# Forgetting attention: head keys, low parts and extra rows loaded from SyncE's queue, and each pair's values loaded behind the value matmuls

## The chip, the cores and the metric

The kernel runs on one core of one Trainium2 chip. The metric is device time in microseconds (us) of that core. A core has TensorE (PE, matrix products into PSUM), VectorE (DVE), ScalarE (ACT) and GpSimd (POOL), which all work out of an on-chip memory of 128 partitions, and SyncE (SP), which here does nothing but start transfers. Each engine works through its own instructions in a fixed order, and an instruction whose inputs or buffers are not ready holds up everything behind it on that engine. Data moves between device memory and the chip by DMA; the transfers of one core share 16 DMA engines. A transfer is started by an instruction on SP, ACT or POOL, and the profile keeps a queue for each of them apart.

## The reference

One inference step of a small decoder: a prompt of 512 tokens and eight sample sequences of four tokens each, 1,024 features wide. A layer with gated linear attention is followed by one with forgetting attention, and each has a feed-forward half before and behind its mixer. The change lies in the forgetting attention. Its keys, values and forget gates are computed once; for the prompt it is ordinary causal attention with a bias from the running sum F of the log forget gates:

```python
s = jnp.einsum('bqhd,bkhd->bhqk', qi, k).astype(jnp.float32) * scale
s = s + (Fi[:, :, :, None] - Ft[:, :, None, :])
s = jnp.where(kpos[None, :] <= qpos[:, None], s, -jnp.inf)
p = jax.nn.softmax(s, axis=-1)
return jnp.einsum('bhqk,bkhd->bqhd', p.astype(v.dtype), v)
```

There are 16 heads of 64 features. A sample sequence attends, with the same formula, over two pages of 128 cached rows, which a page table picks, and over its own four rows. Behind either kind of attention stand the gate `sigmoid(og)` and the output projection `w_o`.

## The kernel before

**The whole.** Nearly all of the run is dense products on PE. Most operands are split into a high and a low part, and each product is made in three passes (high by high, low by high, high by low; L176 to L178), so that float32 accuracy comes out of a faster format ("fp32r" in the profile). The forgetting-attention stage is the function `fox` (L1155 on): it projects queries and gates (`fq`, `fg`), runs the attention loop, and then the output projection (`fwo`). The loop, L1383 to L1409, takes some 146 us of the run.

**The loop.** It has 18 steps. Step i makes the scores and probabilities of prompt head i (`head_probs`), transposes the probabilities of head i-1 (`head_turn`), and in odd steps from 3 on multiplies the values of one pair of heads (`head_values((i-3)//2)`). Woven into it is the attention of the sample sequences, one pair of sequences p in each four steps: `pair_keys` for its first and second sequence (cache blocks b = 2p and 2p+1) in the first two of them, `pair_softmax` and `pair_probs` in the others, and in the next four `pair_values` and `pair_out`. So four heads and one pair of sequences make one group, and there are four groups.

**What a pair of heads loads.** Keys, values and gates were written to scratch in device memory earlier in the run. In each even step `pair_loads(kb)` (L1314) loads for one pair of heads, one pair ahead of its use:

- `vq` (L1316, 256 KB): the values, by SP, into one of two buffers.
- `kd` (L1319, 256 KB in each of two transfers of 64 partitions): the high parts of the keys, by POOL, into one of six buffers (`hi_tile`) that the transposed cache keys `kpT` share.
- `kl` (L1321, 296 KB): the low parts of the keys, and ten more rows with the gates' sums, 74 partitions of two rows of 2 KB each, by POOL, two buffers.
- `qe` (L1323, 40 KB): ten extra rows of the queries that go with them, by POOL, two buffers.

ScalarE and, for all pairs but the first, POOL also split that pair's queries here (L1327 to L1329), into `uh` and `ul`. The scores of a head (L1344 to L1346, tiles `fs`) are, for each block of 128 queries, a product with `kd`, a product with `kl` and a product that adds the causal mask; `kd`'s comes first. ScalarE takes the exponential (L1348). Transposes of the probabilities go to PSUM at L1362 and are copied out by ScalarE (L1366) or VectorE (L1368). The value products (L1377, tiles `fo`) read `vq`; their result is gated by VectorE (L1379), rounded by ScalarE (L1380, `uh`), and POOL subtracts to get the low part (L1381, `ul`).

**What a sample sequence loads.** `pair_keys` starts four transfers of 512 KB, all by SP: two pages of keys `kp` (L1234) and two of values `vp` (L1238). PE transposes the keys in 16 products (L1245, tiles `kpT`, over two PSUM buffers that the other transposes share), VectorE (L1250) and ScalarE (L1248) copy them out, and the scores `sp` (L1227, L1258) and, later, the values `so` (L1295, L1298) follow.

**What sets the order.** The program's text gives the dependencies; a scheduler of the language fixes, when the program is built, one order of instructions for each engine, SP's and POOL's starts of transfers included. In the order listings below, the number at the end of a tile's name only tells tiles apart; the digits ahead of it are the pair of heads (`kd4`), the sequence and the page (`kp2_0`), or the head and the block of queries (`fs5_3`).

Of the kernel before, what the change touches and what calls it, by code (L numbers as in the profile page):

```python
# [9 lines left out]
F32 = mybir.dt.float32  # L10
# [8 lines left out]
P = 128  # L19
D = 1024  # L20
NB = 8
# [29 lines left out]
KX = 74  # L51
# [48 lines left out]
def trunk_kernel(ctx: ExitStack, tc: tile.TileContext, a, out, dbg=None, stop=None):  # L100
    nc = tc.nc
    V, S, G, PE, SP = nc.vector, nc.scalar, nc.gpsimd, nc.tensor, nc.sync
# [7 lines left out]
    def mm_bank(name):  # L110
        return pp.tile([P, 512], F32, tag="mm", name=name, bufs=5)
# [11 lines left out]
    def hi_tile(name, dt=F32R):  # L123
        return wp.tile([P, 1056], dt, tag="hi", name=name, bufs=6)
# [874 lines left out]
    vscr = dram.tile([TP, D], F32, name="vscr")  # L999
    khscr = dram.tile([D, TP], F32, name="khscr")  # L1000
    klscr = dram.tile([16, KX, TP], F32, name="klscr")
    qxscr = dram.tile([16, KX - 64, TP], F32, name="qxscr")
# [152 lines left out]
    def fox(after_half):  # L1155
        W = a["fox_w_qg"][0]
        with ExitStack() as es:
# [43 lines left out]
            fa = es.enter_context(tc.tile_pool(name="foxa", bufs=1))  # L1201
# [75 lines left out]
            def pair_probs(p):  # L1277
                x, xn = pst[p][3:5]
                pt_ = aux_bank(f"spT{p}")
                PE.transpose(pt_[:, 0:128], x[:, 0:128], ident)  # L1280
                PE.transpose(pt_[:, 128:256], x[:, 128:256], ident)
                PE.transpose(pt_[:, 256:384], xn[:].rearrange("p a t -> p (a t)"), ident)
                xT = rb[:, 0:512]
                S.copy(xT[:, 0:384], pt_[:, 0:384])
                pst[p].append(xT)

            def pair_values(p):
                vv, xT = pst[p][2], pst[p][5]
                po = xp.tile([P, 512], F32, tag="sp", name=f"so{p}")
                for s2 in range(2):  # L1290
                    for step in range(3):
                        for j in range(4):
                            o = po[32 * j:32 * j + 32, 256 * s2:256 * s2 + 256]
                            if step < 2:
                                PE.matmul(o, lhsT=xT[:, step * P + 32 * j:step * P + 32 * j + 32], rhs=vv[2 * s2 + step][:, 256 * j:256 * j + 256], start=step == 0, stop=False)  # L1295
                            else:
                                r = slice(32 * j, 32 * j + 32)
                                PE.matmul(o, lhsT=xT[r, 256 + 32 * j:288 + 32 * j], rhs=vnew[r, :], start=False, stop=True)  # L1298
                xo = rb[:, 0:512].rearrange("p (a d) -> p a d", d=64)
                V.tensor_tensor(out=xo, in0=po[:].rearrange("p (a d) -> p a d", d=64), in1=cf[:, F_DIAG:F_DIAG + 8].unsqueeze(2).to_broadcast([P, 8, 64]), op=ALU.mult)  # L1300
                o2 = tmp.tile([P, 128], F32, tag="acc", name=f"o2{p}", bufs=2)
                V.tensor_reduce(out=o2[:], in_=xo.rearrange("p (a b) d -> p (b d) a", b=2), axis=AX.X, op=ALU.add)
                pst[p].append(o2)
# [7 lines left out]

            hst = {}

            def pair_loads(kb):  # L1314
                vq = fa.tile([P, 4, P], F32, tag="vq", name=f"vq{kb}", bufs=2)
                SP.dma_start(out=vq[:], in_=vscr[:].rearrange("(t p) d -> p t d", p=P)[:, :, kb * P:(kb + 1) * P])  # L1316
                kd = hi_tile(f"kd{kb}")[:, 0:1024].rearrange("p (e t) -> p e t", e=2)
                for g in range(2):
                    G.dma_start(out=kd[64 * g:64 * g + 64], in_=khscr[kb * P:(kb + 1) * P].rearrange("(e p) t -> p e t", e=2))  # L1319
                kl = fa.tile([KX, 2, TP], F32R, tag="kl", name=f"kl{kb}", bufs=2)  # L1320
                G.dma_start(out=kl[:], in_=klscr[2 * kb:2 * kb + 2].rearrange("e p t -> p e t"))  # L1321
                qx = fa.tile([KX, 2, TP], F32R, tag="qe", name=f"qe{kb}", bufs=2)
                G.dma_start(out=qx[64:KX], in_=qxscr[2 * kb:2 * kb + 2].rearrange("e p t -> p e t"))  # L1323
                qs = (uh[:, kb, 0:TP], ul[:, kb, 0:TP])
                for e in range(2):
                    r, x = slice(64 * e, 64 * e + 64), slice(64 - 64 * e, 128 - 64 * e)
                    S.copy(qs[e][r], qT[r, kb])  # L1327
                    (G if kb else V).tensor_tensor(out=qs[e][x], in0=qT[r, kb], in1=qs[e][r].bitcast(F32), op=ALU.subtract)
                    S.copy(qx[0:64, e], qT[r, kb])  # L1329
                hst["v", kb], hst["k", kb] = vq, (kd, kl, qs, qx)  # L1330

            def head_probs(hd):
                kb, hh = divmod(hd, 2)
                kd, kl, qs, qx = hst["k", kb]
                gb = fa.tile([P, 1280], F32, tag="gb", name=f"gb{hd}", bufs=2)
                mx = fa.tile([P, 3, 4], F32, tag="mx", name=f"mx{hd}", bufs=3)
                for bank in BANKS:
                    ps = mm_bank(f"fs{hd}_{bank[0]}")
                    o = 0
                    for qt in bank:  # L1340
                        n = (qt + 1) * P
                        tq, one = slice(qt * P, (qt + 1) * P), slice(qt, qt + 1)
                        s_, g = ps[:, o:o + n], gb[:, base(qt):base(qt + 1)]
                        PE.matmul(s_, lhsT=qs[hh][:, tq], rhs=kd[:, hh, 0:n], start=True, stop=False)  # L1344
                        PE.matmul(s_, lhsT=qx[0:KX, hh, tq], rhs=kl[:, hh, 0:n], start=False, stop=False)
                        PE.matmul(ps[:, o + n - P:o + n], lhsT=identb[:], rhs=causb[:], start=False, stop=True)  # L1346
                        V.tensor_reduce(out=mx[:, 0, one], in_=s_, axis=AX.X, op=ALU.min)
                        S.activation(g, s_, AF.Exp, bias=mx[:, 0, one], scale=-1.0, accum_out=mx[:, 1, one])  # L1348
                        o += n
                    for qt in bank:  # L1350
                        one, g = slice(qt, qt + 1), gb[:, base(qt):base(qt + 1)]
                        V.reciprocal(out=mx[:, 2, one], in_=mx[:, 1, one])
                        V.tensor_scalar(out=g, in0=g, scalar1=mx[:, 2, one], scalar2=None, op0=ALU.mult)
                hst["g", hd] = gb
# [17 lines left out]
            def head_values(kb):  # L1372
                vq = hst["v", kb]
                po = mm_bank(f"fo{kb}")
                for kt in range(4):
                    for hh in range(2):
                        PE.matmul(po[64 * hh:64 * hh + 64, kt * P:512], lhsT=vq[:, kt, 64 * hh:64 * hh + 64], rhs=hst["p", 2 * kb + hh][kt][:], start=kt == 0, stop=kt == 3)  # L1377
                og = tmp.tile([P, TP], F32, tag="w2", name=f"og{kb}", bufs=1)
                V.tensor_tensor(out=og[:], in0=sg[kb // 2][:, kb % 2], in1=po[:], op=ALU.mult)  # L1379
                S.copy(uh[:, kb, 0:TP], og[:])  # L1380
                G.tensor_tensor(out=ul[:, kb, 0:TP], in0=og[:], in1=uh[:, kb, 0:TP].bitcast(F32), op=ALU.subtract)  # L1381

            sc_ = {}  # L1383
            for i in range(18):
                p, q = divmod(i, 4)
                if i == 0:
                    pair_loads(0)
                if i % 2 == 0 and i < 14:
                    pair_loads(i // 2 + 1)
                if i < 16:  # L1390
                    head_probs(i)
                if p and q == 0:
                    pair_values(p - 1)
                if p < 4 and q == 0:
                    sc_[0] = pair_keys(p, 0)
                if p < 4 and q == 1:
                    sc_[0]()
                    sc_[1] = pair_keys(p, 1)
                if i >= 3 and i % 2:
                    head_values((i - 3) // 2)  # L1400
                if p < 4 and q == 2:
                    sc_[1]()
                    pair_softmax(p)
                if 1 <= i < 17:
                    head_turn(i - 1)
                if p < 4 and q == 3:
                    pair_probs(p)
                if p and q == 1:
                    pair_out(p - 1)  # L1409
            V.tensor_tensor(out=oS[:], in0=oS[:], in1=sgs[:], op=ALU.mult)  # L1410
            halves(uh[:, :, TP:T], ul[:, :, TP:T], oS[:])
            out_proj("fwo", a["fox_w_o"][0], mod(1, 1, 2), after_half)

    fox(after("12", mod(1, 2, 0), mod(1, 2, 1)))
    dump("h4", h[:])
    if stop == "fox":
# [48 lines left out]
```

## Time and profile before

| | us |
|---|---|
| median of three runs | 2459.66 (2458.26 to 2464.04) |
| profiled execution, its own time | 2463.23 |
| its span, first to last instruction | 2461.4 |
| mean granted clock of PE over the span | 0.989 |
| 0 to 1850 us: PE busy | 1805.2 |
| 1850 to 1996 us, the attention loop: PE busy | 128.1 of 146 |
| 1996 to 2461 us: PE busy | 458.2 |

All times of one instruction and all waits come from the one profiled execution; the median is over separate runs. In the list of waits a row gives the engine and line that waited, what it waited for, the total in us, how many times, and the longest. A row of a timeline has the start, the duration, the engine (SPq is SP's queue), line, operation, output and inputs, and in brackets how long the engine stood idle before it and for whom. A row of a table by stretches has the stretch, its length, the busy time of PE, PE's weight loads, VectorE, ScalarE and POOL with the number of their instructions, and then PE's granted clock as a share of full speed, the mean busy share of the 16 DMA engines, and the traffic in GB/s. A row of the transfers has the tile and its source, the queue, the count, the size of one, and the median of the time from the start instruction to the landing.

### The profile page before, as it was taken

To read this page: it belongs to the slowest core of one execution; us is meant where nothing else is said; L and a number is where in the kernel's file an instruction comes from. 1 tells how busy PE (TensorE), PEld (TensorE's weight loads), DVE (VectorE), ACT (ScalarE), POOL (GpSimd) and SP (SyncE) were. 2 spreads that over 40 slices of the span, in tenths; PEclk is the share of its full clock that TensorE was granted. 3 is DMA by queue.
4 is the path that set the end of the run, shared out by engine and by line. 5 is a ranking of instruction groups with operands and counts; after the bars stand their busy time and mean duration, and the time that the engine had idled before them with its cause. 6 is when DMAs were issued, how large, how long until landed. Compare 5 with 4: busy or idle time off the path is not lost. (4 is left out here: it accounts for less than half of the span.)

```text
span 2461.4 us, 48211 instructions
## 1 busy us (share of the span) xinstructions
PE 2391.6 (97%) x20204; PEld 2244.4 (91%) x20204; DVE 1235.5 (50%) x2823; ACT 783.5 (32%) x1431; POOL 289.5 (12%) x448
## 2 busy tenths in 40 slices
PE   7999999999899999999999999999999799999999
PEld 6999999988879999999979999999896579999999
DVE  6343334557656344344585344434847656444433
ACT  4212222344534213222334322222337444222221
POOL 0000000104302010000220000000325220000000
PEclk9999999999999999999999999999999899999999
DMA  9636454213172646554247323322157742222221
GB/s 308 232 126 231 156 178 133 65 48 96 36 215 60 224 145 230 179 176 154 97 125 233 99 66 109 97 92 69 44 109 196 177 129 74 91 88 93 70 85 54
DMA packets 325519, 319.38 MB, mean 130 GB/s; under 512 B 24607, under 2 KB 276349, under 8 KB 325254
## 3 DMA queue, kind: packets, MB, share of 16 engines
q1 hardware_dynamic: 297958, 293.81, 37.4%
q0 software_dynamic: 13776, 11.87, 2.3%
q10 hardware_dynamic: 13568, 10.62, 1.4%
q8 instruction: 159, 2.61, 0.4%
q14 instruction: 58, 0.48, 0.1%
HBM read 298.17 MB, written 18.38 MB: 129 GB/s over the span
## 5 line engine op out<-in xcount | busy, mean ns | idle before, releaser
L176 PE MATMUL pa<-uh,hua 128*128 128x272 f32 x1408 | 409.5, 291 | 2.0 <-ACT uh L386 2.0
L177 PE MATMUL pa<-ul,hua 128*128 128x272 f32 x1408 | 407.7, 290 | 0.4 <-DVE ul L387 0.2
L178 PE MATMUL pb<-uh,lub 128*128 128x272 f32 x1408 | 407.5, 289 | 0.0
L176 PE MATMUL pd<-gh,hwd 128*128 128x272 f32 x1408 | 407.4, 289 | 0.0
L178 PE MATMUL pa<-uh,lua 128*128 128x272 f32 x1408 | 406.6, 289 | 0.0
L176 PE MATMUL pb<-uh,hub 128*128 128x272 f32 x1408 | 405.5, 288 | 0.0
L177 PE MATMUL pb<-ul,hub 128*128 128x272 f32 x1408 | 405.5, 288 | 0.0
L177 PE MATMUL pd<-gl,hwd 128*128 128x272 f32 x1408 | 405.5, 288 | 0.0
L178 PE MATMUL pd<-gh,lwd 128*128 128x272 f32 x1408 | 405.2, 288 | 0.0
L393 DVE SCALAR_TENSOR_TENSOR h<-pd,mods,h 128x272 f32<-128x272 f32 (+1 forms) x384 | 185.2, 483 | 255.6 <-PE pd L178 254.4
L176 PEld LDWEIGHTS pa<-uh,hua 128*128 128x128 f32 x1408 | 265.3, 188 | 15.1 <-issue 6.0
L176 PEld LDWEIGHTS pd<-gh,hwd 128*128 128x128 f32 x1408 | 265.1, 188 | 2.9 <-issue 2.9
L177 PEld LDWEIGHTS pa<-ul,hua 128*128 128x128 f32 x1408 | 265.7, 189 | 1.4 <-DVE ul L387 1.2
L177 PEld LDWEIGHTS pb<-ul,hub 128*128 128x128 f32 x1408 | 266.1, 189 | 0.0
L178 PEld LDWEIGHTS pb<-uh,lub 128*128 128x128 f32 x1408 | 265.8, 189 | 0.0
L176 PEld LDWEIGHTS pb<-uh,hub 128*128 128x128 f32 x1408 | 265.7, 189 | 0.0
L177 PEld LDWEIGHTS pd<-gl,hwd 128*128 128x128 f32 x1408 | 265.5, 189 | 0.0
L178 PEld LDWEIGHTS pd<-gh,lwd 128*128 128x128 f32 x1408 | 265.4, 188 | 0.0
L178 PEld LDWEIGHTS pa<-uh,lua 128*128 128x128 f32 x1408 | 265.4, 188 | 0.0
L446 DVE TENSOR_TENSOR g<-g,pb 128x272 f32<-128x272 f32 x176 | 77.1, 438 | 346.5 <-PE pb L178 346.3
L157 ACT CAST hua<-rua 128x1024 fp32r<-128x1024 f32 x88 | 92.2, 1048 | 462.9 <-PE pd L177 352.0
L398 POOL TENSOR_TENSOR h<-h,gs 128x32 f32<-128x32 f32 x192 | 69.5, 362 | 1230.7 <-DVE gs L396 1214.6
(497 smaller groups left out, 4173.1 us busy)
## 6 DMA issues: line engine op xcount, KB each, us to landing
adaw<-in_w_ada_dram SPq DMA_DIRECT2D x128, 512.0 KB, 6.2
rua<-in_w_ffn_up_dram SPq DMA_DIRECT2D x88, 512.0 KB, 3.8
rub<-in_w_ffn_up_dram SPq DMA_DIRECT2D x88, 512.0 KB, 3.8
rwd<-in_w_ffn_down_dram SPq DMA_DIRECT2D x88, 512.0 KB, 5.3
adah<-in_w_ada_dram SPq DMA_DIRECT2D x16, 512.0 KB, 7.9
adaw<-in_w_ada_kv_dram SPq DMA_DIRECT2D x16, 512.0 KB, 7.3
s<-in_state_gla_dram SPq DMA_DIRECT2D x16, 512.0 KB, 6.2
kp<-in_cache_k_dram SPq DMA_DIRECT2D x16, 512.0 KB, 5.7
```

What stands on the lines that cost most here:

```text
L157: S.copy(hi, src)
L176: PE.matmul(ps, lhsT=wh, rhs=xh, start=first and i == 0, stop=False)
L177: PE.matmul(ps, lhsT=wh, rhs=xl, start=False, stop=False)
L178: PE.matmul(ps, lhsT=wl, rhs=xh, start=False, stop=last and i == n - 1)
L393: V.scalar_tensor_tensor(out=h[:, m, t0:p1], in0=ps[:, 0:n], scalar=mods[:, gate + m, 0:1], in1=h[:, m, t0:p1], op0=ALU.mult, op1=ALU.add)
L398: G.tensor_tensor(out=h[:, m, TP:T], in0=h[:, m, TP:T], in1=st[:], op=ALU.add)
L446: V.tensor_tensor(out=g[:], in0=g[:], in1=pb[:, 0:HA], op=ALU.mult)
```

## The change

The transfers of `kd`, `kl` and `qe` are started by SP in place of POOL. Their tiles have the type fp32r and their source float32; the tiles are now named to the transfer as plain float32, of the same bits, so that nothing has to be converted and SP can start them. The transfer of `vq` leaves `pair_loads` and becomes a function `value_load` of its own: the values of the first two pairs are loaded in step 0, and those of pair (i+1)//2 right behind the value products of pair (i-3)//2, whose buffer they take. Sizes, buffers and all arithmetic are the same. Lines of the changed kernel: `vq` L1317, `kd` L1323, `kl` L1325, `qe` L1327, the scores L1348 to L1350, the transposes of probabilities L1366, the value products L1381; lines up to L1310 keep their numbers.

```diff
--- before.py
+++ after.py
@@ -1311,23 +1311,27 @@
 
             hst = {}
 
+            def value_load(kb):
+                if kb < NB:
+                    vq = fa.tile([P, 4, P], F32, tag="vq", name=f"vq{kb}", bufs=2)
+                    SP.dma_start(out=vq[:], in_=vscr[:].rearrange("(t p) d -> p t d", p=P)[:, :, kb * P:(kb + 1) * P])
+                    hst["v", kb] = vq
+
             def pair_loads(kb):
-                vq = fa.tile([P, 4, P], F32, tag="vq", name=f"vq{kb}", bufs=2)
-                SP.dma_start(out=vq[:], in_=vscr[:].rearrange("(t p) d -> p t d", p=P)[:, :, kb * P:(kb + 1) * P])
                 kd = hi_tile(f"kd{kb}")[:, 0:1024].rearrange("p (e t) -> p e t", e=2)
                 for g in range(2):
-                    G.dma_start(out=kd[64 * g:64 * g + 64], in_=khscr[kb * P:(kb + 1) * P].rearrange("(e p) t -> p e t", e=2))
+                    SP.dma_start(out=kd[64 * g:64 * g + 64].bitcast(F32), in_=khscr[kb * P:(kb + 1) * P].rearrange("(e p) t -> p e t", e=2))
                 kl = fa.tile([KX, 2, TP], F32R, tag="kl", name=f"kl{kb}", bufs=2)
-                G.dma_start(out=kl[:], in_=klscr[2 * kb:2 * kb + 2].rearrange("e p t -> p e t"))
+                SP.dma_start(out=kl[:].bitcast(F32), in_=klscr[2 * kb:2 * kb + 2].rearrange("e p t -> p e t"))
                 qx = fa.tile([KX, 2, TP], F32R, tag="qe", name=f"qe{kb}", bufs=2)
-                G.dma_start(out=qx[64:KX], in_=qxscr[2 * kb:2 * kb + 2].rearrange("e p t -> p e t"))
+                SP.dma_start(out=qx[64:KX].bitcast(F32), in_=qxscr[2 * kb:2 * kb + 2].rearrange("e p t -> p e t"))
                 qs = (uh[:, kb, 0:TP], ul[:, kb, 0:TP])
                 for e in range(2):
                     r, x = slice(64 * e, 64 * e + 64), slice(64 - 64 * e, 128 - 64 * e)
                     S.copy(qs[e][r], qT[r, kb])
                     (G if kb else V).tensor_tensor(out=qs[e][x], in0=qT[r, kb], in1=qs[e][r].bitcast(F32), op=ALU.subtract)
                     S.copy(qx[0:64, e], qT[r, kb])
-                hst["v", kb], hst["k", kb] = vq, (kd, kl, qs, qx)
+                hst["k", kb] = (kd, kl, qs, qx)
 
             def head_probs(hd):
                 kb, hh = divmod(hd, 2)
@@ -1385,6 +1389,8 @@
                 p, q = divmod(i, 4)
                 if i == 0:
                     pair_loads(0)
+                    value_load(0)
+                    value_load(1)
                 if i % 2 == 0 and i < 14:
                     pair_loads(i // 2 + 1)
                 if i < 16:
@@ -1398,6 +1404,7 @@
                     sc_[1] = pair_keys(p, 1)
                 if i >= 3 and i % 2:
                     head_values((i - 3) // 2)
+                    value_load((i + 1) // 2)
                 if p < 4 and q == 2:
                     sc_[1]()
                     pair_softmax(p)
```

The built order changes as follows at the places that matter below. First SP, around the transfers of `kp2`, the cache keys of the second group's first sequence. Before (rows named ISA fetch the page's number from the page table):

```order
L1238 DMA vp1_1_21004<-in_cache_v_dram 128x1024
L1234 ISA
L1234 DMA kp2_0_21303<-in_cache_k_dram 128x1024
L1234 ISA
L1234 DMA kp2_1_21305<-in_cache_k_dram 128x1024
L1316 DMA vq2_21056<-vscr_13797 128x4x128
L1238 ISA
L1238 DMA vp2_0_21307<-in_cache_v_dram 128x1024
```

And now:

```order
L1238 DMA vp1_1_21004<-in_cache_v_dram 128x1024
L1325 DMA kl2_21059<-klscr_13799 74x2x512
L1323 DMA kd2_21056<-khscr_13798 64x2x512 x2
L1327 DMA qe2_21061<-qxscr_13800 10x2x512
L1323 DMA kd3_21217<-khscr_13798 64x2x512 x2
L1317 DMA vq2_21188<-vscr_13797 128x4x128
L1325 DMA kl3_21220<-klscr_13799 74x2x512
L1327 DMA qe3_21222<-qxscr_13800 10x2x512
L1234 ISA
L1234 DMA kp2_0_21301<-in_cache_k_dram 128x1024
L1234 ISA
L1234 DMA kp2_1_21303<-in_cache_k_dram 128x1024
```

The cache keys stood ahead of `vq2`, and right behind the cache values of the sequence before; now `vq2`, `kl3` and `qe3` stand ahead of them. Second, POOL, where the keys of pair 4 were started:

```order
L1321 DMA kl4_21482<-klscr_13799 74x2x512
L1323 DMA qe4_21484<-qxscr_13800 10x2x512
L1319 DMA kd4_21479<-khscr_13798 64x2x512
L1381 TENSOR_TENSOR ul_69<-og1_21447,uh_68 128x512
L1319 DMA kd4_21479<-khscr_13798 64x2x512
L1319 DMA kd5_21640<-khscr_13798 64x2x512 x2
L1321 DMA kl5_21643<-klscr_13799 74x2x512
```

and SP now, at the same place of the program:

```order
L1317 DMA vq3_21449<-vscr_13797 128x4x128
L1325 DMA kl4_21480<-klscr_13799 74x2x512
L1323 DMA kd4_21477<-khscr_13798 64x2x512 x2
L1327 DMA qe4_21482<-qxscr_13800 10x2x512
L1323 DMA kd5_21638<-khscr_13798 64x2x512
L1317 DMA vq4_21609<-vscr_13797 128x4x128
L1323 DMA kd5_21638<-khscr_13798 64x2x512
```

On POOL a subtraction stood between the two halves of `kd4`; on SP they are one behind the other, and the second half of `kd5` has `vq4` ahead of it. Third, PE, at the transposes of `kp2`. Before, from the last values of the sample pair on; four of the 16 transposes (`kpT2_0`) stand some twenty rows further up, among the scores of head 5:

```order
L1295 MATMUL so0_21265<-vp1_1_21004,rb_71 32x256 x4
L1298 MATMUL so0_21265<-vnew_13804,rb_71 32x256 x4
L1245 MATMUL kpT2_1_21319<-cst_74,kp2_0_21303 128x128
L1245 MATMUL kpT2_1_21319<-cst_74,kp2_1_21305 128x128
L1245 MATMUL kpT2_1_21319<-cst_74,kp2_0_21303 128x128
L1245 MATMUL kpT2_1_21319<-cst_74,kp2_1_21305 128x128
L1245 MATMUL kpT2_2_21325<-cst_74,kp2_0_21303 128x128
L1245 MATMUL kpT2_2_21325<-cst_74,kp2_1_21305 128x128
L1245 MATMUL kpT2_2_21325<-cst_74,kp2_0_21303 128x128
L1245 MATMUL kpT2_2_21325<-cst_74,kp2_1_21305 128x128
L1227 MATMUL sp1_21301<-nf_13805,cf_19760 128x260
```

And now:

```order
L1298 MATMUL so0_21263<-vnew_13804,rb_71 32x256 x4
L1350 LDWEIGHTS identb_19755
L1350 MATMUL fs5_0_21377<-causb_19756,identb_19755 128x128
L1381 MATMUL fo1_21436<-pt2_0_21195,vq1_20863 64x512
L1227 MATMUL sp1_21299<-nf_13805,cf_19760 128x260
L1245 MATMUL kpT2_0_21311<-cst_74,kp2_0_21301 128x128
L1245 MATMUL kpT2_1_21317<-cst_74,kp2_0_21301 128x128
L1348 MATMUL fs6_3_21492<-kd3_21217,uh_68 128x512
L1349 MATMUL fs6_3_21492<-kl3_21220,qe3_21222 128x512
L1350 LDWEIGHTS identb_19755
L1350 MATMUL fs6_3_21492<-causb_19756,identb_19755 128x128
L1245 MATMUL kpT2_0_21311<-cst_74,kp2_1_21303 128x128
```

All 16 transposes of `kp2` now stand behind the sample's values, the end of head 5's scores and one value product of pair 1; 14 of them follow one another behind the first scores of head 6.

## The prediction

> **What bounds the kernel now.** I read the page's first and third parts, then the waits of TensorE (PE) between 1850 and 1996 us, which is the attention stage that the change touches, then that stage in stretches, and last the transfers behind its waits.
>
> ```profile
> PE 2391.6 (97%) x20204; PEld 2244.4 (91%) x20204; DVE 1235.5 (50%) x2823; ACT 783.5 (32%) x1431; POOL 289.5 (12%) x448
> q0 software_dynamic: 13776, 11.87, 2.3%
> ...
> PE fs L1344 <- DMA kd<-khscr: 12.7, 2, 6.8
> PE kpT L1245 <- DVE kpT L1250: 1.2, 1, 1.2
> ...
> 1880.00:1911.00 31.00, 30.57 (x243) 19.12 (x242) 24.93 (x83) 19.88 (x55) 9.19 (x11) 1.00 0.82 201
> 1911.00:1917.00 6.00, 0.11 (x1) 0.14 (x1) 1.08 (x4) 2.51 (x7) 3.21 (x3) 0.76 0.48 112
> 1917.00:1948.00 31.00, 30.56 (x238) 19.93 (x238) 23.21 (x78) 17.14 (x48) 5.92 (x8) 0.94 0.84 191
> 1948.00:1955.00 7.00, 0.39 (x1) 0.41 (x2) 2.64 (x2) 2.30 (x6) 3.09 (x3) 0.77 0.42 92
> 1955.00:1996.00 41.00, 40.69 (x319) 24.01 (x317) 27.24 (x86) 19.78 (x53) 2.56 (x2) 0.96 0.38 124
> ```
>
> PE is the bound nearly everywhere: the stretches at 1880, 1917 and 1955 have 0.3 to 0.4 us idle in them. The stage's loss is two holes, 5.89 and 6.82 us, in which the scores of head 8 and of head 12 wait for kd, the keys of pairs 4 and 6. Four heads and one pair of sample sequences (two cache blocks) make a group; without a hole a group takes 31 us. The transfers behind the holes, first on POOL's own timeline, then by landing:
>
> ```profile
> 1897.23 1.44 POOL L1321 DMA_DIRECT2D kl<-klscr  x1 [13.43 <-PE fs L1346]
> 1899.24 0.61 POOL L1319 DMA_DIRECT2D kd<-khscr  x1
> 1902.59 1.28 POOL L1381 TENSOR_TENSOR ul<-og,uh 128x512 fp32r<-128x512 f32 x1 [2.75 <-ACT uh L1380]
> 1903.82 1.90 POOL L1319 DMA_DIRECT2D kd<-khscr  x3
> ...
> kp<-in_cache_k_dram SPq DMA_DIRECT2D x16, 512.0 KB, 5.7
> kd<-khscr POOLq DMA_DIRECT2D x16, 256.0 KB, 12.3
> kl<-klscr POOLq DMA_DIRECT2D x8, 296.0 KB, 13.1
> ```
>
> The second half of kd4 is issued 4.6 us behind the first, because a subtraction that waits for ScalarE stands between them, and a kd of 256 KB needs 12.3 us to land where a kp of 512 KB needs 5.7. What the slow one is made of shows in a stretch in which only the POOL queue moves anything, beside one with only SP's queue:
>
> ```profile
> DMA packets 305, 0.29 MB, mean 72 GB/s; under 512 B 165, under 2 KB 165, under 8 KB 305
> ...
> DMA packets 566, 1.10 MB, mean 366 GB/s; under 512 B 33, under 2 KB 33, under 8 KB 565
> ```
>
> The first is 1839 to 1843 us, the tail of two kl with their kd and qe; the second 1764 to 1767 us, loads of the query weights with rows of the same 2 KB. So a row of 2 KB is not slow in itself: 366 GB/s is to be had, and the tail runs at a fifth of it. I read that as kl sitting on few of the 16 DMA engines.
>
> **What is removed.** The two holes, 12.7 us, and the slow clock behind them:
>
> ```profile
> 1914.00:1922.00 8.00, 5.11 (x28) 3.92 (x32) 2.68 (x7) 1.20 (x4) 0.24 (x1) 0.57 0.23 61
> 1952.00:1959.00 7.00, 4.39 (x17) 3.45 (x18) 2.25 (x7) 0.42 (x1) 0.00 (x0) 0.53 0.23 57
> 1866.00:1870.00 4.00, 3.96 (x17) 2.75 (x17) 2.06 (x7) 2.37 (x5) 3.94 (x6) 0.57 0.66 138
> 1916.89 0.77 PE L1344 MATMUL fs<-kd,uh 128*128 128x512 f32 x1 [5.89 <-DMA kd<-khscr]
> 1921.18 0.48 PE L1344 MATMUL fs<-kd,ul 128*128 128x512 f32 x1
> 1954.61 0.77 PE L1344 MATMUL fs<-kd,uh 128*128 128x512 f32 x1 [6.82 <-DMA kd<-khscr]
> 1958.41 0.54 PE L1344 MATMUL fs<-kd,ul 128*128 128x512 f32 x1
> ```
>
> The same matmul takes 0.77 us instead of 0.48 from 1916.89 to 1921.18 and from 1954.61 to 1958.41: 8.1 us at 0.62 of the pace lose 3.0 us. Will the holes go? kd4 now follows kl4 on SP with nothing else between, at about 1900 us. If kl4 flows for 7 us (below) and two kd of 256 KB at 366 GB/s for 1.4, kd4 is there by 1911. Head 8 was ready for it at 1911.0, and comes later in the changed order (below), at about 1913.5. So both holes close: minus 15.7. Bounds: nothing (they stay) to minus 15.7.
>
> POOL also loses its 32 issues, by the rows above 16 kd of 0.61 us, 8 kl of 1.44 and 8 qe no longer than a kd, in all 26 us; POOL is 12% busy and nothing on PE's list of waits names it, so that is worth nothing. Values one pair earlier are worth nothing either: no row of that list names vq. SP takes 32 issues of 0.38 us; it is the waits in its queue that matter.
>
> **What is added: kp behind vq and kl.** SP works its queue in order. Before, kp2 went out as soon as its buffer was free. Now it stands behind vq2, which waits for the last value matmul of pair 0, and behind kl3, which waits for the last scores of pair 1. The same repeats in each group (kp4, kp6).
>
> ```profile
> 1867.54 0.90 SPq L1234 DMA_DIRECT2D kp<-in_cache_k_dram  x2
> 1879.30 0.38 SPq L1316 DMA_DIRECT2D vq<-vscr  x1
> ...
> 1878.11 1.16 PE L1377 MATMUL fo<-pt,vq 128*64 128x256 f32 x6 [0.26 <-DVE pt L1368]
> 1888.45 1.09 PE L1245 MATMUL kpT<-cst,kp 128*128 128x128 f32 x8
> ...
> L1234 SPq DMA_DIRECT2D kp<-in_cache_k_dram x2: 333/333/333, 1857.4 to 1858.0; - x2
> DMA to landing us min/median/max: 3.2/3.2/3.2
> ```
>
> Let t be the end of the value matmuls, 1879.2 in the first group. PE comes to the transposes of kp at 1888.45 in the old order; in the new one four transposes fall away ahead of it (0.5 us) and a score piece, a value matmul and the sp start come in (0.3, 0.5, 0.5): t+10.1, and the second half of kp 0.85 us later. On the other side kl goes out at t+1.2 and starts 1.0 us later; then it flows, then the two kp at 1.4 us each (512 KB at 366 GB/s), and 0.8 us to the landing (a lone kp lands after 3.2 us, of which 1.4 is flow). How long does kl flow? The lower bound is 296 KB at 366 GB/s, 0.8 us; the upper is its landing on POOL less 1.8, 11.3 us; half of the 72 GB/s tail for each of its two kl gives 8.4. I take 7: near the tail, since the load keeps its shape of 74 partitions, and somewhat under it since SP's 2 KB rows have shown the better pace. That puts kp's second half at t+12.8 against t+10.95: 1.9 us per group, three groups, plus 5.6. By the bounds: nothing to 18.5.
>
> [...]
>
> **What is moved on PE.** Of the 16 transposes of kp2 14 now stand in one piece behind head 6's first scores, over two PSUM buffers (kp4 and kp6 alike, with heads 10 and 14), where before they were spread between the sample's values. The one place of the old trace with such a piece is kp1:
>
> ```profile
> 1866.04 1.68 PE L1245 MATMUL kpT<-cst,kp 128*128 128x128 f32 x8 [1.18 <-DVE kpT L1250]
> ```
>
> There it waits 1.18 us for VectorE's copy, and the clock then falls for 4 us (row 1866 to 1870 above). Three pieces: plus 3.5, bounds 0 to 3.5. Together with the late kp, PE idles some 3 us in 4; I count the slow clock in 1.4 of the three groups at 1.5 us each, plus 2.1, bounds 0 to 4.5.
>
> **The sum:** -15.7 + 5.6 + 3.5 + 2.1 = -4.5 us. The profiled execution took 2463.23 us (span 2461.4), 3.6 over the median of 2459.66. So 2458.7 for it, and 2455.2 for the median. The ends of the bounds, with the holes closed, are -15.7 and +10.8.
>
> **Rivals.** First, *a clean win*: SP's queue spreads kl over all engines and kp is in time. For it: 2 KB rows at 366 GB/s on SP; against it: the load's shape is what it was. Then -15.7 + 3.5 + about 0.7 for a dip: -11.5, 2448.2 us. [...]
>
> Second, *the holes stay where they are*: kd still lands behind kl, and what SP gains in issue time kp gives back. For it: kd's 12 us came mostly while kl was ahead of it; against it: 2.5 us of slack by my count. About 0, 2459.7 us.
>
> Third, *slower*: kl flows on SP as long as on POOL, 11.3 us, and holds up kp in every group. The place is the transposes of kp2, kp4, kp6; each waits 6.2 us, in all 18.5, and every group then dips: -15.7 + 18.5 + 3.5 + 4.5 = +10.8, 2470.5 us. It decides from a flow of about 8.5 us, where three stalls of 3.4 us eat the rest of the gain. For it: kl's median landing of 13.1; against it: part of that is POOL's own issue and other traffic at 0.82 DMA share.
>
> **How the numbers follow.** My forecast 0.50, its own range 2451 to 2460; clean win 0.24; no change 0.16; slower 0.10. A measurement of this kernel tells about 0.3% from no change, 7.4 us: faster is below 2452.3, slower above 2467.0. From the forecast 0.14 falls under 2452.3 and 0.36 between; the clean win is faster; the second rival is the same save 0.02. That makes faster 0.38, same 0.50, slower 0.12. The range, 2444 to 2465, reaches from the whole 15.7 (2459.66 - 15.7) to 5 us of loss: it takes in the clean win and no change, and leaves out most of the slower case.
>
> **What would show it.** Right: in the changed profile PE waits no more for kd, but for kp at L1245, 1 to 3 us three times, and for VectorE's kpT copies about 1 us three times; kl's landing from SP is 8 to 11 us while kd's falls under 8; the scores of head 8 start near 1913 and the stage's value matmuls end near 1991. Wrong toward the clean win: kl lands in under 5 us and L1245 waits for no DMA. Wrong toward slower: kp lands more than 15 us after the value load ahead of it, or the DMA share falls under 0.3 while PE waits for kp.

## The result, and the profile after

The changed kernel takes 2472.29 us (median of six runs, 2469.89 to 2474.95) against 2461.61 us for the kernel before, measured beside it (2458.26 to 2464.04). The ratio is 1.0046 with a 95% interval of 1.0029 to 1.0063: 7 to 16 us slower. Forecast was 2455.2, with a range of 2444 to 2465.

The profiled execution has a span of 2473.2 us. The part that the change touches is the attention loop; here and below it is measured from the first product of L1205 to the first of the output projection `fwo`. As one stretch of the table by stretches (columns as explained with the profile before), the kernel before and then the changed one:

```profile
1850.04:1996.02 145.98, 128.11 (x963) 79.37 (x961) 102.95 (x323) 84.62 (x224) 45.90 (x45) 0.94 0.65 169
```

```profile
1854.69:2007.78 153.09, 136.56 (x962) 80.33 (x961) 101.09 (x323) 84.84 (x225) 26.50 (x21) 0.96 0.55 162
```

The loop is 7.1 us longer. PE's idle time in it hardly changes (17.9 us, now 16.5); its busy time grows by 8.5 us, though the products are the same. What follows the loop takes 465.4 us in both. Ahead of it the changed kernel's execution lost 4.7 us, nearly all from 1745 to 1760 us, where it was granted a clock of 0.66 and the other 1.00 for the same products in the same order; over all executions profiled for this study the loop begins between 1844.3 and 1854.7 us, whatever the kernel, so the loop is what is compared below.

PE's list of waits in the changed kernel, 1840 to 2015 us:

```profile
PE kpT L1245 <- DMA kp<-in_cache_k_dram: 11.1, 4, 4.5
PE kpT L1245 <- DVE kpT L1250: 1.6, 2, 1.2
PE pT L1366 <- DVE pt L1372: 1.3, 1, 1.3
PE fs L1348 <- ACT gb L1352: 0.8, 2, 0.4
```

The wait for `kd` (12.7 us) is gone, and a wait for the cache keys `kp` (11.1 us) stands in its place, once in each of the last three groups (in the first of these in two pieces). Its first occurrence on SP's queue, on PE, and in the traffic from 1884 to 1904 us (the strip gives the busy share of the DMA engines in tenths, the row under it GB/s, in slices of half a microsecond; two rows by stretches follow, the second from the next group):

```profile
1883.12 0.39 SPq L1317 DMA_DIRECT2D vq<-vscr  x1
1883.95 0.23 SPq L1325 DMA_DIRECT2D kl<-klscr  x1
1884.23 0.68 SPq L1327 DMA_DIRECT2D qe<-qxscr  x1
1885.10 0.92 SPq L1234 DMA_DIRECT2D kp<-in_cache_k_dram  x2
```

```profile
1880.72 2.37 PE L1381 MATMUL fo<-pt,vq 128*64 128x512 f32 x14
...
1896.61 0.44 PE L1245 MATMUL kpT<-cst,kp 128*128 128x128 f32 x2 [2.47 <-DMA kp<-in_cache_k_dram]
1897.85 0.97 PE L1245 MATMUL kpT<-cst,kp 128*128 128x128 f32 x6 [0.24 <-DMA kp<-in_cache_k_dram]
```

```profile
DMA  2883697999998999979952111111111000018989
GB/s 67 249 219 84 180 291 274 406 225 242 246 254 209 279 262 221 197 250 311 229 156 74 66 57 49 49 57 49 57 49 49 33 0 0 0 57 156 344 369 393
...
1895.00:1899.00 4.00, 1.97 (x11) 1.23 (x11) 1.26 (x2) 0.14 (x1) 0.00 (x0) 0.94 0.13 54
...
1930.00:1934.00 4.00, 1.36 (x4) 0.30 (x2) 1.95 (x6) 0.00 (x0) 0.00 (x0) 1.00 0.99 253
```

While PE waits in the first of these stretches, a share of 0.13 of the engines is busy, two of 16, and they move 54 GB/s. The 14 others are done: of the 16 landings that the trace records for the first page of `kp`, 14 come from 1888.54 to 1889.28 us and two at 1896.54 and 1896.57, behind the two of `kl` (1895.15 and 1895.34). What is left are those two engines' shares of `kp` and of the `vp` behind it, which had to wait for `kl`. The two pages of `kp` arrive 1.24 us apart, which is an eighth of 512 KB at 54 GB/s (64 KB, 1.2 us).

### The profile page after: what moved, and what is told of

It reads as the page before. It is cut to its first block, busy times and chain, and to the rows that moved or that the text cites. A ratio compares the mean times of both kernels' runs of the same rounds, so it can differ in the third digit from the quotient of the medians.

```text
span 2473.2 us, 48197 instructions
## 1 busy us (share of the span) xinstructions
PE 2406.8 (97%) x20204; PEld 2250.6 (91%) x20204; DVE 1233.9 (50%) x2823; ACT 784.0 (32%) x1431; POOL 264.3 (11%) x416
## 5 line engine op out<-in xcount | busy, mean ns | idle before, releaser
L176 PEld LDWEIGHTS pa<-uh,hua 128*128 128x128 f32 x1408 | 266.1, 189 | 15.3 <-issue 6.0
```

Of the source, the lines that this page charges most:

```text
L176: PE.matmul(ps, lhsT=wh, rhs=xh, start=first and i == 0, stop=False)
```

## The experiments

Eight kernels were run, one of them twice. Times in us; the loop as above; ratios are to the kernel before, measured beside each.

| kernel | median | ratio, 95% interval | loop | PE busy in it | waits for transfers |
|---|---|---|---|---|---|
| before | 2461.6 | | 146.0 | 128.1 | kd 12.7 |
| the change | 2472.3 | 1.0046 (1.0029 to 1.0063) | 153.1 | 136.6 | kp 11.1 |
| loads alone on SP | 2472.8 | 1.0044 (1.0024 to 1.0064) | 156.9 | 137.9 | kp 12.0, kd 1.4 |
| change, kl cut 64 + 10 | 2456.0 | 0.9968 (0.9953 to 0.9983) | 136.7 | 130.2 | none |
| change, kl cut 37 + 37 (two runs) | 2511.4 | 1.0189 (1.0162 to 1.0215) | 192.0 | 150.6 | qe (and kl) 25.6, kp 11.4 |
| change, kp first | 2459.0 | 0.9983 (0.9962 to 1.0005) | 141.1 | 129.5 | kp 3.5, kd 1.6 |
| change, both repairs | 2457.3 | 0.9983 (0.9968 to 0.9999) | 140.2 | 130.2 | none |
| before, kl cut 64 + 10 | 2444.6 | 0.9917 (0.9886 to 0.9949) | 128.0 | 122.8 | none |
| the same, timed again | 2443.2 | 0.9927 (0.9912 to 0.9943) | 128.2 | 122.8 | none |
| before, kl cut 37 + 37 | 2472.0 | 1.0036 (1.0016 to 1.0055) | 153.7 | 130.5 | kd 19.5 |
| before, kl cut 64 + 10, kp turned late | 2458.3 | 0.9989 (0.9975 to 1.0004) | 138.0 | 130.1 | kp 4.9 |

**How kl is cut, on SP's queue.** The first edit to the changed kernel; the second has 37 in place of 64.

```diff
-                SP.dma_start(out=kl[:].bitcast(F32), in_=klscr[2 * kb:2 * kb + 2].rearrange("e p t -> p e t"))
+                for r in (slice(0, 64), slice(64, KX)):
+                    SP.dma_start(out=kl[r].bitcast(F32), in_=klscr[2 * kb:2 * kb + 2, r].rearrange("e p t -> p e t"))
```

> The changed kernel, with kl loaded in two transfers, of its first 64 partitions and of the last 10; nothing else differs, and the built orders of SP and PE are those of the changed kernel save for single rows. Attention loop here and below: from the first product of L1205 to the first of fwo, 146.0 us before, 153.1 in the changed kernel. Theory A (kl of 74 partitions sits on two of the 16 DMA engines, and kp's rows on those two queue behind it): kl lands in 3 to 5 us instead of 10, PE's wait for kp at L1245 falls from 11.1 us to under 4, the loop to 139 to 144, the time 9 to 14 us under the changed kernel, under the kernel before too. Rival B (kp is late because it is started behind vq and kl, which wait for PE; how the rows are spread makes no difference): the wait stays at 9 to 13 us, the time within 3 us of the changed kernel.

> As the run before, same bytes, same number of transfers and the same built order, but cut into 37 and 37 partitions. 37 is prime; if the number of engines is the largest up to 16 that divides the number of partitions, each half runs on one engine, and both on the same one. Theory A: kl needs about 20 us, kp's share on that engine comes some 9 us later in each of three groups, the loop grows to 175 to 205 us and the time by 20 to 50 us over the changed kernel. Rival B, and the plain explanation that two smaller transfers are faster than one: as the run before, no longer than the changed kernel.

The built orders of the two are the same on PE and SP; bytes and number of transfers are too. With 64 + 10 PE waits for no transfer any more and the clock stays at full speed (loop row, first fence); the loop of 136.7 us and a time 16 us under the changed kernel are better than theory A expected. With 37 + 37 the loop is 55 us longer; the second fence has its loop, PE's waits and the traffic from 1895 to 1915 us:

```profile
1846.79:1983.52 136.73, 130.16 (x962) 76.92 (x961) 100.27 (x323) 84.86 (x225) 26.53 (x21) 1.00 0.59 181
```

```profile
1849.19:2041.15 191.96, 150.56 (x962) 88.77 (x960) 99.00 (x323) 84.72 (x224) 26.20 (x21) 0.85 0.41 132
...
PE fs L1350 <- DMA qe<-qxscr: 25.6, 6, 5.4
PE kpT L1245 <- DMA kp<-in_cache_k_dram: 11.4, 7, 9.1
...
DMA  0000000358998989479997300000000000000000
GB/s 25 25 25 25 25 25 25 102 102 197 328 393 311 324 295 238 197 315 414 365 361 270 139 25 25 25 25 29 25 25 33 25 25 25 25 33 25 0 0 0
```

The traffic beside the bursts is 25 GB/s, half of what the tail of the 74-partition load moved (54), and the pace of one row of 2 KB after the other at the 0.084 us that such a row of `kl` first took in the changed kernel's trace (24 GB/s): one engine where that was two. The products that wait read both `kl` and `qe`; `qe` only stands last behind `kl` on that queue. So theory A is right on SP. In the changed kernel's trace the landings behind a start (for `kl` and `qe` without one more right at the end of the starting instruction) are 16 for each transfer of 128 or of 64 partitions in the loop, two for `kl` with its 74 and ten for `qe` with its 10; and eight of those of the `qe` started at 1884.23 us come by 1886.49, its last two at 1895.43 and 1895.52, behind `kl`'s two. So the transfers behind the narrow one ended with the engines that the narrow one held. These counts, and the one engine for 37 partitions, are what the expectation for 37 + 37 supposed; what another number of partitions gives is not shown. Rival B falls, since kp's place in the queue was not touched here.

**The same cuts on POOL's queue, in the kernel before.**

```diff
-                G.dma_start(out=kl[:], in_=klscr[2 * kb:2 * kb + 2].rearrange("e p t -> p e t"))
+                for r in (slice(0, 64), slice(64, KX)):
+                    G.dma_start(out=kl[r], in_=klscr[2 * kb:2 * kb + 2, r].rearrange("e p t -> p e t"))
```

> The kernel before, with the same cut of kl into 64 and 10 partitions, all on POOL as it was. Theory A: the two holes at head 8 and head 12, 12.7 us, were kd's rows behind kl's on two engines; they shrink to under 3 us together, kd lands in 6 to 9 us instead of 12.3, the loop falls from 146 to 130 to 136, the time by 9 to 15 us. Rival C (the holes come from POOL: its subtraction between the halves of kd4, and its slow issue): the holes stay at 9 us or more, and with eight more starts on POOL become no shorter; time within 3 us of before.

> The kernel before with kl in two transfers on POOL, of 37 and 37 partitions in place of 64 and 10; the built order of PE is the same, row for row, and of POOL it has the same starts. Theory A (engines by the divisor of the partitions, on POOL too): each half on a single engine, kd's rows on those wait behind them, the waits for kd or kl come to 15 us or more in sum, loop 145 to 185 us. Rival: on POOL it was the cut into two transfers as such that closed the holes, whichever way; loop within 4 us of 128.

First the kernel with 64 + 10 (its loop, and from the transfers of 1820 to 2060 us the landings), then with 37 + 37:

```profile
1850.03:1978.05 128.02, 122.80 (x962) 75.66 (x960) 99.10 (x323) 84.46 (x224) 44.11 (x51) 1.00 0.69 193
...
kd<-khscr POOLq DMA_DIRECT2D x16, 256.0 KB, 5.4
kl<-klscr POOLq DMA_DIRECT2D x8, 256.0 KB, 5.2
kl<-klscr POOLq DMA_DIRECT2D x8, 40.0 KB, 4.8
```

```profile
1847.91:2001.58 153.67, 130.51 (x963) 81.25 (x961) 101.46 (x323) 85.29 (x225) 54.42 (x51) 0.92 0.65 161
...
PE fs L1345 <- DMA kd<-khscr: 19.5, 3, 9.4
...
kd<-khscr POOLq DMA_DIRECT2D x16, 256.0 KB, 16.0
```

`kd` was not touched in either, and lands after 5.4 us with `kl` cut 64 + 10, 12.3 with `kl` whole (kernel before) and 16.0 with 37 + 37. So on POOL, too, the shape of `kl` decides how late `kd` comes. How many engines carry `kl` there is not shown: the trace records 16 landings for each of POOL's transfers in the loop, whatever its shape, and from 1839 to 1843 us of the kernel before, with two `kl` under way, the busy share was 0.35, not the 0.13 of SP's two engines. With 64 + 10 both holes are gone, though POOL's subtraction still stands between the halves of `kd4` and POOL has eight more starts: rival C falls. Loop and time fall further than theory A expected. The order of PE's products is that of the kernel before but for single rows, so the 18.0 us by which the loop shrinks can be split: idle time falls by 12.7 us (17.9 to 5.2), and busy time by 5.3, which is slow clock (0.94 to 1.00). Not all of that clock belongs to the holes. Product by product, 3.5 us are lost behind the two holes, and 1.8 in the first group, ahead of any wait for `kd`: that is the stretch from 1866 to 1870 us, with a clock of 0.57, which the prediction shows behind a wait of 1.18 us for VectorE. So the holes with the slow clock behind them are worth 16.2 us. This kernel is faster than both kernels of the study; the second timing gives 0.9927.

> The same kernel as in the run with kl cut into 64 and 10 on POOL, timed in five rounds beside the kernel before, for its ratio: 0.990 to 0.995 expected from 18 us less in the attention loop (0.9927 of 2461).

**kp ahead of vq and kl on SP.** `kl` whole; the starts of `kp` become a function that is called a step earlier for the first sequence of each group:

```diff
+                if i == 0:
+                    key_pages(0)
+                if p < 4 and q == 1:
+                    key_pages(2 * p + 1)
+                if q == 3 and p < 3:
+                    key_pages(2 * p + 2)
                 if i == 0:
                     pair_loads(0)
```

> The changed kernel, kl whole (74 partitions), but the transfers of kp for the first sequence of each group are written one step earlier and for the second at the start of their step, so that on SP kp2, kp4 and kp6 stand ahead of vq2, vq4, vq6 and of kl3, kl5, kl7. Theory A and rival B agree that PE's wait for kp falls under 3 us, since kp no longer has that kl ahead of it. By A kd4 and kd6 keep kl4 and kl6 ahead of them on two engines, and kp4 and kp6 add to it: a wait for kd of 0 to 6 us comes back; loop 136 to 144. By B alone nothing is late any more: loop 131 to 136.

```profile
1850.74:1991.83 141.09, 129.54 (x963) 77.40 (x961) 101.66 (x323) 85.31 (x225) 26.58 (x21) 1.00 0.61 176
...
PE kpT L1250 <- DMA kp<-in_cache_k_dram: 3.5, 5, 1.2
PE fs L1353 <- DMA kd<-khscr: 1.6, 1, 1.6
```

The wait for `kp` falls from 11.1 to 3.5 us (under 3 was expected), and a wait for `kd` of 1.6 us comes back; the loop is where theory A put it. The better place in the queue took 7.6 of the 11.1 us of waiting for `kp`; with `kl` cut 64 + 10 there was none.

**What is left between 128.0 and 136.7.** With `kl` cut, the loads on SP still cost 8.7 us against the same loads on POOL, at full clock and with no wait for a transfer: 1.3 us of idle time and 7.4 us of busy time. Two kernels test where that comes from, the changed one with both repairs, and the one on POOL with only PE's transposes moved:

```diff
                 def scores():
+                    if s2 == 0:
+                        turn()
                     for kb in range(2):
```

Here `turn()` holds the 16 transposes and their copies, which stood in `pair_keys` before; for the second sequence it is still called there.

> The changed kernel with both repairs: kl in two transfers of 64 and 10 partitions, and kp ahead of vq and of the second kl of each group on SP. So far, with kl cut this way and no wait for any transfer, the attention loop took 128.0 us with the loads on POOL (PE busy 122.9) and 136.7 with the loads on SP (PE busy 130.2, clock at full in both). Theory O (the order of PE's products costs the rest: in the built order of POOL's kernel the sample scores sp are left for another tile 19 times, in that of SP's 28 times, here 26; the value products fo 16, 20 and here 17 times): PE busy 126 to 129 us, loop 131 to 135. Rival T (what is left is waiting for transfers that the list of waits doesn't name; with kp first it goes): loop 127 to 130. Rival S (loads started by SP slow PE down wherever they stand): busy 130, loop 135 to 138. In every case no wait for kp or kd over 1 us.

> The kernel before with kl cut into 64 and 10 on POOL (loop 128.0, PE busy 122.9), and the transposes of the first sequence's cache keys in each group written just ahead of their scores, a step later; the loads stay where they are. The built order then has the 16 transposes of kp4 and of kp6 behind the sample's values and broken up by fo and sp, leaves sp 24 times and fo 21 times for another tile. Theory O: with no load moved to SP, PE's busy time grows to 126 to 130 us and the loop to 131 to 136. Rivals T and S: PE's order alone costs nothing, busy 122 to 124, loop within 2 us of 128.

The loops, of both repairs and of the transposes turned late, and for each the groups of the sample scores (`sp`, L1258 in the kernel before) and of the value products (`fo`), with busy time and the mean of one:

```profile
1844.30:1984.51 140.21, 130.19 (x962) 77.45 (x961) 103.68 (x323) 85.32 (x225) 26.59 (x21) 1.00 0.59 178
...
L1387 PE MATMUL fo<-pt,vq 128*64 128x512 f32 (+3 forms) x128 | 27.3, 444 | 0.0
L1263 PE MATMUL sp<-kpT,qx 128*32 128x260 f32 x128 | 15.3, 393 | 0.5 <-DVE kpT L1255 0.5
```

```profile
1847.63:1985.67 138.04, 130.14 (x962) 77.06 (x960) 98.56 (x323) 84.25 (x224) 43.91 (x51) 0.99 0.63 179
...
L1387 PE MATMUL fo<-pt,vq 128*64 128x512 f32 (+3 forms) x128 | 27.7, 446 | 0.0
L1267 PE MATMUL sp<-kpT,qx 128*32 128x260 f32 x128 | 15.7, 397 | 0.0
```

The same groups with `kl` cut 64 + 10, on POOL and then on SP; each with sample scores of one sequence as its timeline lists them:

```profile
L1378 PE MATMUL fo<-pt,vq 128*64 128x128 f32 (+3 forms) x128 | 25.2, 443 | 0.0
L1258 PE MATMUL sp<-kpT,qx 128*32 128x260 f32 x128 | 12.2, 390 | 0.5 <-DVE kpT L1250 0.5
...
1901.65 1.08 PE L1258 MATMUL sp<-kpT,qx 128*32 128x260 f32 x16
```

```profile
L1382 PE MATMUL fo<-pt,vq 128*64 128x128 f32 (+3 forms) x128 | 28.6, 446 | 0.0
L1258 PE MATMUL sp<-kpT,qx 128*32 128x260 f32 x128 | 15.7, 394 | 0.5 <-DVE kpT L1250 0.5
...
1888.16 0.63 PE L1258 MATMUL sp<-kpT,qx 128*32 128x260 f32 x2
1889.63 0.65 PE L1258 MATMUL sp<-kpT,qx 128*32 128x260 f32 x8
1890.74 0.64 PE L1258 MATMUL sp<-kpT,qx 128*32 128x260 f32 x6
```

With the transposes turned late, no load has left POOL, and yet PE's busy time is 130.1 us against 122.8. At most 1.7 of these 7.3 us are clock (it was granted 0.50 from 1865.7 to 1869.1 us, behind two waits for `kp`, and 1.00 in the rest of the loop); the order does the rest, so rivals S and T fall and theory O stands. Its size was missed upward: with both repairs busy time is 130.2 (126 to 129 expected) and the loop 140.2 (131 to 135; 3.5 more than with the cut alone, as PE waits 4.8 us for VectorE's copies of `kpT` in place of 2.8), and the late transposes' loop is 138.0 (131 to 136), with 4.9 us of waits for `kp` that were not foreseen. The groups show what the order does. One `sp` product takes 0.39 to 0.40 us in every kernel, but its form in the profile is `128*32` (`128*64` for `fo`, `128*128` for the scores' product with `kd`), and neighbours run side by side. In the run of 16 the trace has four starting within 0.02 us, the next four 0.22 us later, and so on: four steps, done in 1.08 us, where 16 times 0.39 would be 6.2. In the other order the runs of 2, 8 and 6 start by ones, fours and threes, six steps in all, and take 0.63, 0.65 and 0.64 us; and behind the last step of such a run a product of another shape starts after some 0.32 us, not 0.22. All 128 take 12.2 us in the order of the kernel before and 15.7 in the changed order; `fo` 25.2 and 28.6. These two groups grow by 6.9 us, the whole by 7.4; as groups overlap with their neighbours, this says where the time is, and is not an exact sum. The number of broken runs doesn't size the loss: `sp` is left for another tile 28 times in one kernel and 24 in another, with 15.7 us in both. The number of steps comes nearer: `sp` needs 42 with `kl` cut on POOL, 50 with it cut on SP and 52 with the transposes turned late. How much is fewer products side by side, and how much the change from one shape to another, was not separated.

**The two halves of the change.** The kernel with the loads on SP and `vq` left in `pair_loads`:

```diff
             def pair_loads(kb):
+                value_load(kb)
...
-                    value_load((i + 1) // 2)
```

> Only the first half of the change: kd, kl (whole) and qe on SP, vq left in pair_loads. The other half alone, vq behind the value products with the loads on POOL, was not run: its built order is row for row that of the kernel before, on PE, SP and POOL. The built order of the half that is run has PE as in the changed kernel, and SP the same save for the places of single vq. Expected: as the changed kernel, wait for kp at L1245 9 to 13 us, loop 151 to 155 us; if the move of vq does part of the harm, the loop is under 150.

```profile
1850.33:2007.18 156.85, 137.89 (x963) 81.33 (x961) 100.35 (x323) 84.94 (x225) 26.52 (x21) 0.95 0.53 157
...
PE kpT L1245 <- DMA kp<-in_cache_k_dram: 12.0, 4, 5.0
PE fs L1349 <- DMA kd<-khscr: 1.4, 1, 1.4
```

The time is that of the whole change (2472.8 and 2472.3), the loop 3.8 us longer, 1.9 over the range expected, with the wait for `kd` not expected. So the loads on SP make the whole loss, and the move of `vq` gives a little back at most (the medians don't tell the two kernels apart); without the loads on SP it changes no order at all.

## Why the prediction was wrong, point by point

**The holes close: right.** No wait for `kd` is left. The step that read `kl` as "sitting on few of the 16 DMA engines" was right too: for SP the traffic shows it (a share of 0.13, 54 GB/s), for POOL the way in which the landing of `kd` follows the cut of `kl` (5.4, 12.3 and 16.0 us). The slow clock behind the holes, put at 3.0 us, is 3.5, so this term was -16.2 where -15.7 was forecast.

**kp behind vq and kl: right in mechanism, half the size.** Forecast 5.6 us, measured 11.1 (2.7, 4.5 and 3.9 where 1.9 each was forecast). What failed is the sizing of `kl`: from its start to its end 8.0 us were counted (1.0 and 7), and by the trace's records of single rows the last row of 2 KB on its engines ended 10.9, 12.2 and 11.5 us behind the start in the three groups. On its two engines a row of 2 KB took 0.084 us at first, but 0.146 (median) from 1887.5 to 1893.5 us, while the 14 others were busy, too (mostly 9 tenths in the strip; 0.99 from 1930 to 1934 us, ahead of the 4.5 us wait), and 0.085 again from 1894.5 us, when they had nothing left. The forecast of 7 us had no such slowing in it. The pages of `kp` behind it were even faster than forecast, 1.24 us each against 1.4. PE came to `kp` where forecast, or a little later: 1896.61 less 2.47 is 1894.14, 11.0 us after the value products' end (1880.72 and 2.37, 1883.1), against 10.1 to 10.95.

**What is moved on PE: the step that failed.** It was priced by VectorE's copies, 3.5 us, and a clock that falls behind them and the late `kp`, 2.1 in all. Waits for the copies of the cache keys hardly grew: 2.3 us at `kpT`, `sp` and `pT` against 2.0 before. The slow clock costs 6.4 us (busy time 136.6 against 130.2 with `kl` cut and the same order but for single rows): 5.1 behind the three waits for `kp`, and 1.3 in the first group, where the kernel before loses 1.8. And the order of the products costs 8.7 us, 6.9 of which show in the two groups of narrow products. The prediction weighed the moved products only for when PE reaches `kp` (0.5, 0.3 and 0.5 us); for their own time there was no term in the sum at all.

**The sum with what was measured:** the kernel before takes 146.0. Less 16.2 for the holes, and less 1.8 for its slow clock in the first group, that is 128.0. Plus 8.7 for the order, plus 15.3 for `kp` (waits of 11.1 and 5.1 of slow clock, less 0.9 of other waits), and plus 1.0 for the changed kernel's own first group, it is 153.1 but for rounding. That is +7.1 where -4.5 was forecast. The first group is chance, as far as is known: PE waits 1.24 us for VectorE there in the changed kernel and 1.25 in two others with the same order (the loads alone, and `kl` cut 64 + 10 on SP), and only the first shows a slow clock behind it:

```profile
1870.76 1.60 PE L1245 MATMUL kpT<-cst,kp 128*128 128x128 f32 x8 [1.24 <-DVE kpT L1250]
...
1870.00:1874.00 4.00, 3.22 (x13) 2.00 (x14) 3.97 (x9) 2.81 (x5) 3.79 (x3) 0.65 1.05 195
```

**The rivals.** The third, slower, named the right place and came nearest (2470.5 to 2472.3), but its number is near by luck: it had 18.5 us of waits for `kp` and no cost of order. Its sign was there, a DMA share of 0.13 while PE waits for `kp`. The clean win fell because `kl` kept to two engines on SP's queue, the second rival because no wait for `kd` is left. The loads' move from POOL brought nothing of its own: with `kl` cut, PE waits for no load on either queue, and the loop is 128.0 us with the loads on POOL and 136.7 with them on SP.

**What stays open:** the medians differ by 10.7 us and the two profiled loops by 7.1, the lower end of the interval. Which of the broken runs cost most was not measured, nor why a wait of 1.2 us is followed by a slow clock in some executions only.

## What to carry to other kernels

Look at the partition count of each transfer before its queue: one on few engines (here `kl`, 74 partitions and two engines on SP) held up the wide transfers behind it, and cutting it at 64 was worth 18 us here where moving it to another queue cost 11. When a change lets a scheduler reorder PE, compare the busy time of groups of narrow form (here `128*32` and `128*64`): the reorder here cost 8.7 us, 7.4 of it busy time, which appears in no list of waits. And price the hole together with the slow clock behind it, here 12.7 and 3.5 us.

## What the runs showed of the hardware that was not expected

- Products of the form `128*32` ran up to four side by side: 16 in one run took 1.08 us, 0.39 each; an order that breaks the runs cost 3.5 us over 128 of them, and 3.4 over 128 of the form `128*64`.
- The clock: behind two holes of 5.9 and 6.8 us 3.5 us were lost to slow products, behind three of 2.5, 4.5 and 3.9 us 5.1. The length of the last wait does not decide by itself: behind waits of 1.18 and 1.24 us for VectorE the clock fell to 0.57 (1866 to 1870 us, kernel before) and 0.65 (above), while four loops with waits up to 1.6 us stayed at 1.00 (loop rows of 64 + 10 on either queue, of kp first, and of both repairs).
- Rows of a narrow transfer took longer while the other engines were busy: 0.146 us for 2 KB on the two engines of `kl`, against 0.084 before and 0.085 behind that stretch.
- POOL took longer to start a transfer of 37 partitions (or of 74, 1.44 us) than one of 64 or 10. From its timelines, first 64 + 10, then 37 + 37, two starts each:

```profile
1895.45 1.19 POOL L1322 DMA_DIRECT2D kl<-klscr  x2 [8.70 <-PE fs L1347]
```

```profile
1899.57 2.89 POOL L1322 DMA_DIRECT2D kl<-klscr  x2 [13.55 <-PE fs L1347]
```

  So 0.6 us a start against 1.45. The quicker two carry 256 and 40 KB, the slower two 148 KB each, so it isn't the bytes; what in the shape decides is not shown.
